# Streaming the first FFN's opening weights and the conditioning rows through one six-slot ring, with the first block accumulated row by row in eight PSUM banks

## The chip, the cores and the metric

The kernel runs on one Trainium2 chip, as one program on all eight NeuronCores (two dies of four). The metric is device time in microseconds of the slowest core. A program on all eight cores has a second, slower state in some executions, in which one die shows a lower granted clock (in one slow run of the changed kernel die 0 had 0.93 and the time was 1721.6 us). "Fast runs" means the rest. Ratios, means over cores and profiles use fast runs alone; the medians below count slow runs too.

TensorE is the matmul engine, ScalarE does activations, VectorE elementwise arithmetic, GpSimd simple elementwise work and casting DMAs, and SyncE issues plain DMAs. SBUF is a core's working memory, and PSUM, in eight banks, takes what TensorE writes. In profile lines they are PE, ACT, DVE, POOL and SP.

## The reference, cut to what matters

The block is a macaron: half an FFN, a token mixer, half an FFN. Each sub-layer is preceded by an RMS norm whose scale and shift come from a conditioning vector `c`.

```python
cc = jax.nn.silu(c)
mod = (cc @ w_ada[l] + b_ada[l]).reshape(b, N_ADA, D_MODEL)    # 9 vectors of 1024
sh1, sc1, gt1, sh2, sc2, gt2, sh3, sc3, gt3 = ...
h = rms_norm(x, g_ffn1[l]) * (1 + sc1) + sh1                   # modulated norm
x = x + 0.5 * gt1 * swiglu(h, w_ffn1_in[l], w_ffn1_out[l])     # first FFN, 1024 -> 2 x 2816 -> 1024
# ... token mixer (chunked attention and pooling), then the second FFN in the same form
```

Each core holds 2048 tokens and a halo of 512, as five blocks of 512 columns. All are transposed, so that the 1024 features lie on partitions, as eight tiles (`kt`) of 128. x, the weights and the conditioning matrix are float32 in HBM. Matmuls are bf16.

## The kernel before

Every instruction goes through a small recording layer, which finds dependences and sets semaphores. Each engine runs its own list in order. An instruction that waits also holds back everything behind it on its engine. (In the trace of the kernel before, ScalarE waits 13.19 us, until 80.91, for an x block that it is to square, and a Silu queued behind starts only at 82.82.)

A norm has a statistics part (`stats`: squares on ScalarE, column sums by matmul with a matrix of ones, Ln and Exp on ScalarE) and an apply part (`ap`, one per tile: a multiply on VectorE, then an add on ScalarE for even tiles and on VectorE for odd ones). Its output, `h`, is kept for each block as `H[b]`, the input of the FFN's matmuls:

```python
def norm_parts(b, sub, mode, out=None):
    ...                                            # cut
    def sq(p):
        return lambda: P.act(SQ[p % 2][:, :, :], x[:, 2 * p:2 * p + 2, :], AF.Square)
    def ln():
        P.act(r, sbk, AF.Ln, bias=EPSC[:, 0:1])
        P.act(r, r, AF.Exp, scale=-0.5)
    def ap(kt):
        def f():
            t = TMP[kt % 2]
            P.stt(t, x[:, kt, :], DER[:, 3 * sub, kt:kt + 1], r, ALU.mult, ALU.mult)
            if mode == "act" or (mode == "mix" and kt % 2 == 0):
                P.act(h[:, kt, :], t, AF.Identity, bias=DER[:, 3 * sub + 1, kt:kt + 1])
            else:
                P.ts(h[:, kt, :], t, DER[:, 3 * sub + 1, kt:kt + 1], ALU.add)
        return f
```

At the start, two x blocks and 16 rows of `w_ada` are loaded through SyncE's queue. Each row is turned into one scale or shift by a VectorE dot product. The first `w1i` tiles are loaded by GpSimd, which casts to bf16 in the DMA, and each of these loads waits for a given dot, so that it does not steal bandwidth from the rows. The third x block waits for the last of these loads:

```python
for i in range(16):
    dots.append(ada_dot(aorder[i], ADA_R[i % 6]))
    if i + 6 < 16:
        ada_load(aorder[i + 6], ADA_R[i % 6], "d_a%d" % (i % 6))
    ...                                            # cut: scale/shift, early H tiles of blocks 0 and 1
pre1, body1 = ffn(w1i, w1o, 0, [0, 1, 2, 3, 4], True, ..., startup=[dots[1], dots[7], dots[11], dots[13]], ...)
pre1()
last = pre1()
P.load("sp", XB[1][:, :, :], xT[2], "d_x2", deps=last)
```

A `unit` is 16 matmuls into a pair of PSUM banks (8 for each half of the SwiGLU), a Silu and a multiply. In "group 0" each of the five blocks has four units. The norms of blocks 2 to 4 are woven between the units of the blocks before them (`norm_slots`):

```python
def unit(k, jj, b, spread=None):
    ...                                            # cut: 16 matmuls into bank 2*pi and 2*pi+1
    P.act(s, bank(2 * pi), AF.Silu)
    P.tt(ACTB[jl][:, b, :], s, bank(2 * pi + 1), ALU.mult)

for bi, b in enumerate(blocks):                    # group 0
    for k in range(2):
        for jj in range(2):
            unit(k, jj, b, spread if bi == k == jj == 0 else None)
            side["g0"](bi, 2 * k + jj)             # parts of the norms of later blocks
```

## Time and profile before

| | before |
|---|---|
| time, median of 3 runs | 1636.98 us (1635.83 to 1641.05) |
| spans of the eight cores in the profiled run | 1622.4 to 1638.0 us |
| TensorE busy | 1517.3 us, 93% |

The page's first lines and its queue table (queue, kind: packets, MB written, share of the time of 16 DMA engines):

```profile
span 1638.0 us, 20449 instructions; the slowest of 8 cores (1622.4 to 1638.0 us)
...
PE 1517.3 (93%) x7085; PEld 669.1 (41%) x7085; DVE 821.3 (50%) x1300; ACT 478.9 (29%) x615; POOL 96.2 (6%) x193
...
q0 software_dynamic: 31184, 59.91, 22.4%
q1 hardware_dynamic: 14688, 58.30, 11.0%
```

Queue 0 casts float32 to bf16, so 59.91 MB written are 119.8 MB read.

The chain of waits of the kernel before, followed back from the last instruction, cut to 60 to 150 us (start, length, what was waited for or run; L179 and so on are the recording layer's lines):

```profile
58.42 6.86 DMA arena<-w1i
65.52 15.31 DMA arena<-xT
80.91 1.07 ACT arena L185
...
89.05 1.28 ACT L186
...
91.76 1.28 ACT L185
```

Read it as a relay. The chain waits 6.9 us for a casting weight load, then 15.3 us for the third x block (issued only at 65.5), then it follows ScalarE's norm work. ACT L186 and L185 with 1.28 us are loads of the activation table: Ln and Silu need different tables, so each norm swaps twice.

The stretches table of the kernel before, some of its rows (per stretch: length, busy us and count for each engine, then the granted TensorE clock, the DMA share and GB/s):

```profile
core 3: us, PE busy (x) PEld busy (x) DVE busy (x) ACT busy (x) POOL busy (x), PEclk, DMA share, GB/s
...
70.00:80.00 10.00, 0.15 (x1) 0.00 (x0) 0.00 (x0) 0.00 (x0) 0.00 (x0) 0.74 1.00 260
80.00:90.00 10.00, 7.89 (x30) 3.10 (x31) 1.37 (x2) 5.92 (x7) 0.00 (x0) 0.74 1.04 304
90.00:100.00 10.00, 9.56 (x46) 4.13 (x43) 5.00 (x8) 6.79 (x10) 0.00 (x0) 1.00 0.61 233
110.00:120.00 10.00, 7.88 (x37) 3.36 (x35) 7.11 (x11) 5.86 (x8) 0.00 (x0) 1.00 0.18 53
140.00:150.00 10.00, 6.58 (x22) 2.23 (x20) 5.96 (x10) 2.52 (x4) 0.00 (x0) 0.83 0.29 107
```

TensorE does next to nothing from 70 to 80 us, and from about 146 us on it is full but for some 2 us at the second FFN's entry and holes in the mixer. So the front is what a change can improve.

### The profile page before, as it was taken

The numbers are of one execution on the slowest core, as the hardware profiler recorded it, in microseconds if no ns is written. First come the engines' busy times: TensorE is split into PE (matmuls) and PEld (weight loads), VectorE is DVE, ScalarE is ACT, GpSimd is POOL, SyncE is SP. The second block draws the span as 40 slices with busy tenths as digits, with TensorE's granted clock in tenths as the row PEclk, the third lists the DMA queues.
The fourth block names the chain that finished last, engine by engine and source line by source line (L and its number), as shares of the span: only waits on it lengthen the run. The fifth ranks groups of instructions, "written<-read, shape, count | busy, mean of one in ns | idle before, by whom it ended". The sixth has DMA issues, their size and how long they took to land.

```text
span 1638.0 us, 20449 instructions; the slowest of 8 cores (1622.4 to 1638.0 us)
## 1 busy us (share of the span) xinstructions
PE 1517.3 (93%) x7085; PEld 669.1 (41%) x7085; DVE 821.3 (50%) x1300; ACT 478.9 (29%) x615; POOL 96.2 (6%) x193
## 2 busy tenths in 40 slices
PE   1488999999999999988699988799999999999999
PEld 0133444444444444343244433244434444444444
DVE  3446736537346346756555456455356261624326
ACT  3363010110110114657744157643250101010110
POOL 0101000010010000000100000111000000001000
PEclk9899999999999999999999999899999999999999
DMA  9844353151361344020144530344304313104005
GB/s 278 185 144 103 67 129 78 39 135 39 90 130 32 80 116 89 1 38 15 21 71 77 90 53 1 51 71 67 71 3 75 52 27 58 27 14 85 13 1 205
DMA packets 45970, 119.50 MB, mean 73 GB/s; under 512 B 4144, under 2 KB 4272, under 8 KB 45360
## 3 DMA queue, kind: packets, MB, share of 16 engines
q0 software_dynamic: 31184, 59.91, 22.4%
q1 hardware_dynamic: 14688, 58.30, 11.0%
q8 instruction: 60, 0.98, 0.2%
q14 instruction: 38, 0.31, 0.1%
HBM read 169.70 MB, written 8.39 MB: 109 GB/s over the span
## 4 chain that ended last, share of the span: by engine, by line
PE 82%; ACT 5%; DVE 5%; DMA 4%; issue 3%; SPq 0%; DVEq 0%; ACTq 0%; POOL 0%; POOLq 0%
PE ps L179 82%; ACT arena L185 3%; DVE arena L189 2%; DVE arena L194 1%; DMA arena<-w_ada 1%; ACT arena L186 1%; DMA arena<-w_ap 1%; DMA arena<-xT 1%; DVE arena L196 1%; SPq L215 0%; DMA arena<-w1i 0%; DVE arena L209 0%; DVE arena L201 0%; ACT L185 0%; ACT L186 0%
## 5 line engine op out<-in xcount | busy, mean ns | idle before, releaser
L179 PE MATMUL ps<-arena 128*128 128x512 bf16 (+3 forms) x7085 | 1517.3, 377 | 116.8 <-ACT arena L185 55.6
L179 PEld LDWEIGHTS ps<-arena 128*128 128x128 bf16 (+1 forms) x7085 | 669.1, 98 | 964.5 <-issue 212.0
L185 ACT ACTIVATE arena<-ps 128x512 bf16<-128x512 f32 (+4 forms) x368 | 270.3, 744 | 870.5 <-PE ps L179 862.1
L189 DVE TENSOR_TENSOR arena<-arena,ps 128x512 bf16<-128x512 bf16 (+1 forms) x230 | 175.2, 762 | 563.8 <-PE ps L179 484.6
L194 DVE SCALAR_TENSOR_TENSOR arena<-ps,arena 128x512 f32<-128x512 f32 (+1 forms) x410 | 315.8, 774 | 125.6 <-PE ps L179 71.1
L185 ACT ACTIVATE arena<-arena 128x1024 bf16<-128x1024 f32 (+2 forms) x105 | 95.2, 929 | 42.8 <-DMA arena<-xT 17.6
L189 DVE TENSOR_TENSOR arena<-arena 128x512 bf16<-128x512 bf16 (+10 forms) x191 | 89.9, 494 | 25.5 <-ACT arena L185 17.3
L196 DVE SCALAR_TENSOR_TENSOR arena<-arena 128x1024 f32<-128x1024 f32 x72 | 87.8, 1219 | 26.4 <-DMA arena<-w_ada 25.5
L186 ACT ACTIVATE arena<-arena 128x512 bf16<-128x512 f32 (+1 forms) x84 | 57.5, 714 | 121.1 <-DVE arena L194 96.4
L194 DVE SCALAR_TENSOR_TENSOR arena<-arena 128x512 f32<-128x512 f32 (+2 forms) x114 | 78.8, 727 | 6.2 <-ACT arena L186 2.9
L215 POOL DMA_DIRECT2D arena<-w1i x28 | 17.8, 636 | 517.2 <-PE ps L179 463.3
L189 DVE TENSOR_TENSOR arena<-ps,arena 64x512 bf16<-64x512 f32 x32 | 22.0, 689 | 35.0 <-ACT arena L185 31.5
L215 POOL DMA_DIRECT2D arena<-w3i x24 | 16.2, 677 | 380.3 <-PE ps L179 380.3
L215 POOL DMA_DIRECT2D arena<-w_in x28 | 19.8, 707 | 306.8 <-PE ps L179 289.4
L186 ACT ACTIVATE arena<-ps,arena 128x1024 f32<-128x1024 f32 (+1 forms) x32 | 29.6, 925 | 25.5 <-PE ps L179 25.3
L185 ACT ACT_TABLE_LOAD x14 | 18.0, 1283 | 43.6 <-PE ps L179 36.5
L201 DVE TENSOR_SCALAR arena<-arena 128x512 bf16<-128x512 f32 (+2 forms) x45 | 19.9, 443 | 5.7 <-DMA arena<-cst 1.1
L186 ACT ACT_TABLE_LOAD x12 | 15.4, 1283 | 16.3 <-PE ps L179 16.2
L212 POOL MEMSET arena<- 64x128 bf16 x64 | 11.8, 197 | 132.1 <-ACT arena L185 132.1
L201 DVE TENSOR_SCALAR arena<-ps,arena 128x512 bf16<-128x512 f32 (+2 forms) x25 | 15.7, 644 | 7.2 <-PE ps L179 7.0
L209 DVE CAST arena<-ps 128x256 bf16<-128x256 f32 x32 | 12.1, 419 | 7.4 <-PE ps L179 7.4
L209 DVE COPY arena<-arena 128x16 f32<-128x16 f32 (+2 forms) x35 | 6.0, 171 | 8.2 <-ACT arena L185 6.8
(14 smaller groups left out, 51.1 us busy)
## 6 DMA issues: line engine op xcount, KB each, us to landing
arena<-w_ada SPq DMA_DIRECT2D x72, 512.0 KB, 4.4
arena<-w_in POOLq DMA_DIRECT2D x28, 512.0 KB, 6.7
arena<-w3i POOLq DMA_DIRECT2D x20, 512.0 KB, 6.8
arena<-w1i POOLq DMA_DIRECT2D x16, 512.0 KB, 8.9
outT<-arena SPq DMA_DIRECT2D x16, 512.0 KB, 2.9
arena<-xT SPq DMA_DIRECT2D x3, 2048.0 KB, 23.4
arena<-w1o POOLq DMA_DIRECT2D x10, 512.0 KB, 15.1
arena<-w3o POOLq DMA_DIRECT2D x10, 512.0 KB, 9.8
```

The lines of the kernel that those rows point to most:

```text
L179: return self.op("pe", lambda e: e.matmul(out, lhsT=lhsT, rhs=rhs, start=start, stop=stop), reads=[lhsT, rhs], writes=[out])
L185: return self.op("act", lambda e: e.activation(out=out, in_=in_, func=func, scale=scale), r, [out])
L186: return self.op("act", lambda e: e.activation(out=out, in_=in_, func=func, bias=bias, scale=scale), r, [out])
L189: return self.op(eng, lambda e: e.tensor_tensor(out=out, in0=in0, in1=in1, op=op), [in0, in1], [out])
L194: return self.op("dve", lambda e: e.scalar_tensor_tensor(out=out, in0=in0, scalar=scalar, in1=in1, op0=op0, op1=op1), r, [out])
L196: return self.op("dve", lambda e: e.scalar_tensor_tensor(out=out, in0=in0, scalar=scalar, in1=in1, op0=op0, op1=op1, accum_out=accum), r, ...
L201: return self.op(eng, lambda e: e.tensor_scalar(out=out, in0=in0, scalar1=s1, scalar2=None, op0=op0), r, [out])
L209: return self.op(eng, lambda e: e.tensor_copy(out=out, in_=in_), [in_], [out])
L212: return self.op(eng, lambda e: e.memset(out, v), [], [out])
L215: return self.op(q, lambda e: e.dma_start(out=out, in_=in_), [], [out], deps, sem)
```

## The change

The intent has four parts. (1) One hardware queue carries x blocks 0 and 1 and then, through a ring of six slots, eight weight tiles in float32 and the 16 conditioning rows. ScalarE casts the weight tiles. (2) As each pair of rows becomes a scale and a shift, one H tile of block 0 is made and all four units of block 0 take their eight matmuls of that tile at once, in all eight PSUM banks. After the last row, block 0 is nearly done. Dummy ("warm") matmuls fill the gaps. (3) The norms of blocks 2 to 4 do their four squares together, with four buffers. (4) Their odd-tile adds go to GpSimd, in the second FFN too. (One more edit, not in this list: the conditioning dots among these norms, which prepare later scales and shifts, stand behind units 0, 2 and 3 of a block and no longer behind 0, 1 and 2.)

The diff, cut to its core:

```diff
+    RING = [view(o_h + 16384 + 4096 * i, F32, (D,)) for i in range(6)]
+    tiles = [w1i[half * NJ + j] for j in range(4) for half in (0, 1)]
+    tiles += [w_ada[8 * (1 - s_) + k] for k in range(8) for s_ in (0, 1)]
+    def tile_load():
+        n = tn[0]
+        if n < len(tiles):
+            tn[0] += 1
+            P.load("sp", RING[n % 6], tiles[n], "d_a%d" % (n % 6))
...
+    for j in range(4):
+        for half in range(2):
+            n = 2 * j + half
+            P.act(piece((0, 2)[j // 2] + half)[:, j % 2, :], RING[n % 6], AF.Copy)
+            tile_load()
+    P.act(EPSC[:, 1:2], EPSC[:, 0:1], AF.Silu)
     for i in range(16):
-        dots.append(ada_dot(aorder[i], ADA_R[i % 6]))
+        slot = RING[(8 + i) % 6]
+        P.stt(slot, slot, 1.0, CB[:, :], ALU.mult, ALU.mult, accum=MRAW[...])
+        if i == 0:
+            warm(10, 0, True, P.q["dve"][-1])
+        tile_load()
         if i % 2 == 1:
...
+            for b in range(2):
+                P.act(H[b][:, kt, :], XR[b][:, kt, :], AF.Identity, scale=..., bias=...)
+            for j in range(4):
+                for half in range(2):
+                    P.mm(bank(2 * j + half), piece(...)[:, j % 2, kt * 128:(kt + 1) * 128], H[0][:, kt, :],
+                         kt == 0, kt == 7)
+            if kt < 7:
+                warm(5, 7, False)
...
-                if mode == "act" or (mode == "mix" and kt % 2 == 0):
+                if mode == "act" or (mode != "dve" and kt % 2 == 0):
                     P.act(h[:, kt, :], t, AF.Identity, bias=DER[:, 3 * sub + 1, kt:kt + 1])
                 else:
-                    P.ts(h[:, kt, :], t, DER[:, 3 * sub + 1, kt:kt + 1], ALU.add)
+                    P.ts(h[:, kt, :], t, DER[:, 3 * sub + 1, kt:kt + 1], ALU.add, "pool" if mode == "pool" else "dve")
...
-    N1 = norm_slots(2, 3, 0, 2)
+    for b in range(2, 5):
+        st, ap = norm_parts(b, 0, "pool", sq4, tmp4)
+        at = (4, 5, 5, 6, 7) if b == 2 else (4 * b - 5, 4 * b - 4, 4 * b - 4, 4 * b - 3, 4 * b - 2)
+        for v, f in zip(at, (st[:4], st[4:], ap[:3], ap[3:6], ap[6:])):
+            N1.setdefault(v, []).extend(f)
...
-    P.load("sp", XB[1][:, :, :], xT[2], "d_x2", deps=last)
+    for b in range(2, 5):
+        for p in range(4):
+            P.load("sp", XB[b - 1][:, 2 * p:2 * p + 2, :], xT[b][:, 2 * p:2 * p + 2, :], "d_x%d%d" % (b, p))
...
```

More of the change, by code (lines that the diff above doesn't have):

```diff
@@ L417, in build_nc, with norm_parts @@
     nctr = [0]
-    def norm_parts(b, sub, mode, out=None):
+    def norm_parts(b, sub, mode, sqs=None, tmps=None):
         i = nctr[0]
@@ L424, in norm_parts @@
         x = xb(b)
-        h = H[b] if out is None else out
+        h = H[b]
+        sqs = SQ if sqs is None else sqs
+        ns = len(sqs)
+        tmps = TMP if tmps is None else tmps
         def sq(p):
-            return lambda: P.act(SQ[p % 2][:, :, :], x[:, 2 * p:2 * p + 2, :], AF.Square)
+            return lambda: P.act(sqs[p % ns][:, :, :], x[:, 2 * p:2 * p + 2, :], AF.Square)
         def st(p):
@@ L432, in f @@
                 for q in range(2):
-                    P.mm(sbk, ONES[:, :], SQ[p % 2][:, q, :], p == 0 and q == 0, p == 3 and q == 1)
+                    P.mm(sbk, ONES[:, :], sqs[p % ns][:, q, :], p == 0 and q == 0, p == 3 and q == 1)
             return f
@@ L441, in f @@
             def f():
-                t = TMP[kt % 2]
+                t = tmps[kt % len(tmps)]
                 P.stt(t, x[:, kt, :], DER[:, 3 * sub, kt:kt + 1], r, ALU.mult, ALU.mult)
-                if mode == "act" or (mode == "mix" and kt % 2 == 0):
+                if mode == "act" or (mode != "dve" and kt % 2 == 0):
                     P.act(h[:, kt, :], t, AF.Identity, bias=DER[:, 3 * sub + 1, kt:kt + 1])
                 else:
-                    P.ts(h[:, kt, :], t, DER[:, 3 * sub + 1, kt:kt + 1], ALU.add)
+                    P.ts(h[:, kt, :], t, DER[:, 3 * sub + 1, kt:kt + 1], ALU.add, "pool" if mode == "pool" else "dve")
             return f
         stats = [sq(0), sq(1), st(0), sq(2), st(1), sq(3), st(2), st(3), ln]
+        if ns == 4:
+            stats = [sq(p) for p in range(4)] + [st(p) for p in range(4)] + [ln]
         return stats, [ap(kt) for kt in range(8)]
@@ L471, in build_nc @@
     P.load("sp", CB[:, :], cb_d, "d_cb")
-    ADA_R = [view(o_h + 16384 + 4096 * i, F32, (D,)) for i in range(6)]
+    RING = [view(o_h + 16384 + 4096 * i, F32, (D,)) for i in range(6)]
     XR = [view(base + 17408, F32, (8, TB)), view(o_w + 4 * 4096, F32, (8, TB))]
-    aorder = [8 * (1 - s) + k for k in range(8) for s in (0, 1)]
+    tiles = [w1i[half * NJ + j] for j in range(4) for half in (0, 1)]
+    tiles += [w_ada[8 * (1 - s_) + k] for k in range(8) for s_ in (0, 1)]
+    tn = [0]
+    def tile_load():
[3 more added lines that the diff above has]
+            P.load("sp", RING[n % 6], tiles[n], "d_a%d" % (n % 6))
     for b in range(2):
@@ L477, in build_nc @@
             P.load("sp", xb(b)[:, 2 * p:2 * p + 2, :], xT[b][:, 2 * p:2 * p + 2, :], "d_x%d%d" % (b, p))
-        if b == 0:
-            for i in range(2):
-                ada_load(aorder[i], ADA_R[i], "d_a%d" % i)
-    for i in range(2, 6):
-        ada_load(aorder[i], ADA_R[i], "d_a%d" % i)
+    for i in range(6):
+        tile_load()
     P.memset(ONES[:, :], 1.0 / 1024.0)
@@ L492, in build_nc, with warm @@
     P.ts(B1, CST[:, 16:24], 1.0, ALU.add)
-    def warm(n):
+    def warm(n, bk, start, after=None):
         for _ in range(n):
-            P.mm(bank(5), WARM[:, 0:128], WARM[:, :], True, True)
-    def xr_parts(b):
+            P.op("pe", lambda e: e.matmul(bank(bk), lhsT=WARM[:, 0:128], rhs=WARM[:, :], start=start, stop=start),
+                 [WARM[:, :]], [bank(bk)], [after])
+    for b in range(2):
         st, _ = norm_parts(b, 0, "mix")
-        r = RSTD[b]
-        return st, [lambda kt=kt: P.tt(XR[b][:, kt, :], xb(b)[:, kt, :], r, ALU.mult) for kt in range(8)]
-    st0, xr0 = xr_parts(0)
-    st1, xr1 = xr_parts(1)
-    seq = {0: st0[:2], 1: st0[2:3] + st0[3:6], 2: st0[6:], 3: xr0[0:2], 4: xr0[2:4] + st1[:2], 5: xr0[4:6] + st1[2:6],
-           6: xr0[6:8] + st1[6:], 7: xr1[0:2], 8: xr1[2:4], 9: xr1[4:6], 10: xr1[6:8]}
-    dots = []
-    def early(b, kt):
-        P.act(H[b][:, kt, :], XR[b][:, kt, :], AF.Identity, scale=DER[:, 0, kt:kt + 1], bias=DER[:, 1, kt:kt + 1])
-    eseq = {7: [(0, 0), (0, 1), (0, 2), (0, 3)], 9: [(0, 4)], 11: [(0, 5), (1, 0), (1, 1)], 13: [(0, 6), (1, 2), (1, 3)],
-            15: [(0, 7), (1, 4), (1, 5), (1, 6), (1, 7)]}
-    for i in range(16):
-        dots.append(ada_dot(aorder[i], ADA_R[i % 6]))
-        if i + 6 < 16:
-            ada_load(aorder[i + 6], ADA_R[i % 6], "d_a%d" % (i % 6))
+        for f in st:
+            f()
+        for kt in range(8):
+            P.tt(XR[b][:, kt, :], xb(b)[:, kt, :], RSTD[b], ALU.mult)
+    for j in range(4):
[4 more added lines that the diff above has]
+    P.act(EPSC[:, 1:2], EPSC[:, 0:1], AF.Silu)
+    P.ts(EPSC[:, 2:3], EPSC[:, 0:1], EPSC[:, 0:1], ALU.add, "pool")
+    for i in range(16):
+        slot = RING[(8 + i) % 6]
+        P.stt(slot, slot, 1.0, CB[:, :], ALU.mult, ALU.mult, accum=MRAW[:, 8 * (1 - i % 2) + i // 2:8 * (1 - i % 2) + i // 2 + 1])
+        if i == 0:
+            warm(10, 0, True, P.q["dve"][-1])
+        tile_load()
         if i % 2 == 1:
@@ L520, in build_nc @@
             P.tt(DER[:, 1, kt:kt + 1], MRAW[:, kt:kt + 1], CST[:, 8 + kt:9 + kt], ALU.add)
-        for f in seq.get(i, []):
-            f()
-        for b, kt in eseq.get(i, []):
-            early(b, kt)
+            for b in range(2):
+                P.act(H[b][:, kt, :], XR[b][:, kt, :], AF.Identity, scale=DER[:, 0, kt:kt + 1], bias=DER[:, 1, kt:kt + 1])
+            for j in range(4):
+                for half in range(2):
+                    P.mm(bank(2 * j + half), piece((0, 2)[j // 2] + half)[:, j % 2, kt * 128:(kt + 1) * 128], H[0][:, kt, :],
+                         kt == 0, kt == 7)
+            if kt < 7:
+                warm(5, 7, False)
     ada_j = [16]
@@ L540, in build_nc, with ffn, wi_load @@
     G0 = [sum(GS[:g]) for g in range(5)]
-    def ffn(w_i, w_o_, sub, blocks, first, side, wi_slots, wo_odd, startup=None, tail=None, spread=None):
+    def ffn(w_i, w_o_, sub, blocks, side, wi_slots, wo_odd, started=False, tail=None):
         chunks = [(g, c) for g in range(5) for c in range((GS[g] + 1) // 2)]
         nload = [0]
-        def wi_load(split=None):
+        def wi_load():
             k = nload[0]
@@ L554, in wi_load @@
             sa, sb = wi_slots[k % 2]
-            if split is not None:
-                return [P.load("pool", piece(s)[:, jj:jj + 1, :],
-                               w_i[o + j0 + jj:o + j0 + jj + 1].rearrange("j p c -> p j c"),
-                               "d_w%d" % s if jj == 0 else "d_wy%d" % s, deps=[split[2 * k + jj]])
-                        for jj in range(nt) for s, o in ((sa, 0), (sb, NJ))]
             for s, o in ((sa, 0), (sb, NJ)):
@@ L562, in ffn, with unit @@
         ucnt = [0]
-        def unit(k, jj, b, spread=None):
+        def unit(k, jj, b, done=None):
             g, c = chunks[k]
@@ L567, in unit @@
             jl = 2 * c + jj
-            pi = nextpair()
-            order = [(s, o, kt) for s, o in ((sa, 0), (sb, 1)) for kt in range(8)]
-            if spread is not None:
-                order.sort(key=lambda x: x[2])
-            for s, o, kt in order:
-                P.mm(bank(2 * pi + o), piece(s)[:, jj, kt * 128:(kt + 1) * 128], H[b][:, kt, :], kt == 0, kt == 7)
-                if spread is not None and o == 1:
-                    spread(kt)
+            pi = nextpair() if done is None else done
+            if done is None:
+                for s, o in ((sa, 0), (sb, 1)):
+                    for kt in range(8):
+                        P.mm(bank(2 * pi + o), piece(s)[:, jj, kt * 128:(kt + 1) * 128], H[b][:, kt, :], kt == 0, kt == 7)
             s = SA[ucnt[0] % 2]
@@ L607, in pre @@
         def pre():
-            return wi_load(startup)
+            return wi_load()
         def body():
-            if startup is None:
+            if started:
+                nload[0] = 2
+                for u in range(4):
+                    unit(u // 2, u % 2, blocks[0], done=u)
+            else:
                 wi_load()
@@ L614, in body @@
             for bi, b in enumerate(blocks):
+                if bi == 0 and started:
+                    continue
                 for k in range(2):
                     for jj in range(2):
-                        unit(k, jj, b, spread if bi == k == jj == 0 else None)
+                        unit(k, jj, b)
                         side["g0"](bi, 2 * k + jj)
@@ L642, in ffn, with norm_slots @@
         return pre, body
-    def norm_slots(first, nb, sub, start):
+    def norm_slots(first, nb, sub, start, lo=0):
         slots = {}
@@ L649, in put @@
             slots.setdefault(v, []).extend(f)
-        free_at = 0
+        free_at = lo
         for q in range(nb):
@@ L654, in norm_slots @@
             v = [v0, v0 + 1, v0 + 2]
-            st, ap = norm_parts(first + q, sub, "mix")
+            st, ap = norm_parts(first + q, sub, "pool")
             put(v[0], st[0], st[1])
@@ L667, in g0_norms @@
             f()
-    N1 = norm_slots(2, 3, 0, 2)
+    N1 = {}
+    sq4 = SQ + [view(o_w + 4 * 4096 + 2048 * i, BF16, (2, TB)) for i in range(2)]
+    tmp4 = TMP + [view(o_w + 5 * 4096 + 2048 * i, F32, (TB,)) for i in range(2)]
+    for b in range(2, 5):
[3 more added lines that the diff above has]
+            N1.setdefault(v, []).extend(f)
     sd = Side()
-    pend = []
-    for b in range(1, 5):
-        pend.append(None)
     ucount = [0]
@@ L678, in g0_1 @@
         g0_norms(4 * bi + u, N1)
-        if bi >= 2 and u < 3:
+        if bi >= 2 and u != 1:
             ada_step()
@@ L710, in tail_1 @@
                 tl[b].q.extend(ng)
-    pre1, body1 = ffn(w1i, w1o, 0, [0, 1, 2, 3, 4], True, dict(g0=g0_1, g0end=g0end_1, unit=unit_1, op=lambda: None),
-                      [(0, 1), (2, 3)], (4, 5), startup=[dots[1], dots[7], dots[11], dots[13]], tail=tail_1,
-                      spread=lambda kt: warm(5) if 2 <= kt <= 6 else None)
-    pre1()
-    last = pre1()
-    P.load("sp", XB[1][:, :, :], xT[2], "d_x2", deps=last)
-    for i in range(2):
-        ada_load(16 + i, ada_slot(16 + i), "d_b%d" % i)
-    for b in range(3, 5):
-        P.load("sp", XB[b - 1][:, :, :], xT[b], "d_x%d" % b)
-    P.load("pool", WPG[:, :, :], w_pg.rearrange("(g c) d -> c g d", c=128), "d_wpg", deps=[dots[15]])
+    _, body1 = ffn(w1i, w1o, 0, [0, 1, 2, 3, 4], dict(g0=g0_1, g0end=g0end_1, unit=unit_1, op=lambda: None),
+                   [(0, 1), (2, 3)], (4, 5), started=True, tail=tail_1)
+    for b in range(2, 5):
+        for p in range(4):
+            P.load("sp", XB[b - 1][:, 2 * p:2 * p + 2, :], xT[b][:, 2 * p:2 * p + 2, :], "d_x%d%d" % (b, p))
+        if b == 2:
+            for i in range(2):
+                ada_load(16 + i, ada_slot(16 + i), "d_b%d" % i)
+    P.load("pool", WPG[:, :, :], w_pg.rearrange("(g c) d -> c g d", c=128), "d_wpg", deps=[P.q["dve"][-1]])
     body1()
@@ L1036, in build_nc @@
     sl = fr[:2] + rest
-    pre2, body2 = ffn(w3i, w3o, 2, [1, 2, 3, 4], False, dict(g0=g0_2, g0end=sd2.drain, unit=lambda: None, op=lambda: None),
+    pre2, body2 = ffn(w3i, w3o, 2, [1, 2, 3, 4], dict(g0=g0_2, g0end=sd2.drain, unit=lambda: None, op=lambda: None),
                       [(sl[0], sl[1]), (sl[2], sl[3])], (sl[4], sl[5]), tail=tail_2)
```

## The prediction

> **What bounds the kernel now.** The page has TensorE busy 1517 of 1638 us (93%); the stretches table shows it full from about 146 us on, but for 2 us near 1200 to 1220. Only the front is worth anything. There TensorE is busy 9.2 us of 60 to 70, 0.15 of 70 to 80, 7.9 of 80 to 90, 6.6 of 140 to 150. The chain of waits names, in order: conditioning rows by DMA to 31 us; VectorE dots and XR products to 57; DMA of w1i to 65; DMA of the third x block from 65.5 to 80.9 (held until the last w1i load is issued); then a ScalarE/VectorE norm chain of 19 to 20 us a block (table loads at 91.8, 110.7, 130.6). Block 0's last unit ends at about 87 us, block 4's H is complete at 146, group 0 ends at about 158.5.
>
> **What changes.**
> - Removed: eight casting w1i loads that waited for dots. They now stream ahead of the rows. By the queue table a casting byte read costs the DMA engines no more (59.9 MB written, so 119.8 read, took 22.4%; 58.3 MB plain took 11.0%). The Trainium skill, "DMA: Bandwidth & Descriptors" (SWDGE vs HWDGE vs iDMA), has casts only on the GpSimd path; hence 8 ScalarE casts, about 1.0 us each, hidden under DMA.
> - Moved: two x blocks, 8 weight tiles and 16 rows are 17.4 MB in one queue. The trace had moved 11.0 MB by 40 us and then ran at 318 GB/s: last row at about 60 us (estimate). First row at about 35; two dots with scale and shift take 3.53 us (54.72 to 58.25), eight pairs 28: last dot at about 63, against 60.8. Six slots hold 10 us of stream, issue to landing takes 4.4: the ring should not starve.
> - Gained: after the last row 8 matmuls remain, not 3 units, and the third x block lands at about 68, not 81. Block 1 starts at about 67, against 87.
> - Norms of blocks 2 to 4: four squares (4 us), 8 statistics matmuls (1.75), Ln with table (2.0), Exp 0.63, 8 applies, odd adds on GpSimd. The skill's "GPSIMD Engine Reference" (Engine selection) calls one-input ops there roughly line-rate; estimate 0.8 to 1.2 us against 0.49 on VectorE; the trace of before has none. Walking the in-order queues with the trace's durations (silu 0.6, multiply 0.69, apply 0.7, add 0.72, dot 1.3), H of blocks 2, 3, 4 is complete 27, 45 and 64 us after the last dot: still 18 to 19 us a block, not TensorE's 16, as Silu and Ln still swap tables.
> - Group 0 then ends at 63+77=140, against 158.5.
>
> **On the critical path.** Nearly all 18 us. About 1 us may come or go at the second FFN, whose adds also go to GpSimd. Warm matmuls fill gaps: free.
>
> **Prediction:** 1637-18 = 1619 us, 8 in 10 between 1611 and 1627. Over 2% faster 0.04 (TensorE-bound from 67 us would save only about 30 us), within 2% 0.95, over 2% slower 0.01.
>
> **Right or wrong if** (timeline): last row's dot at 60 to 66 us; silu within 3 us of it; no TensorE hole over 5 us between 66 and 80; block 2's squares at 69 to 74; first output projection at 136 to 145; table loads still 18 to 20 us apart; the rest unchanged within 2 us.
>
> **What would make it wrong.** The ring starves: last dot after 68. GpSimd adds over 2 us, or VectorE slowed beside them. The w1o loads delay x. Better: blocks come every 16 us, up to 28 us saved. Worse: block 1 waits over 2 us for pair 0's eviction.

## The result, and the profile after

| | before | changed |
|---|---|---|
| median, same rounds | 1638.53 us | 1634.51 us |
| ratio of fast runs | | 0.9973, 95% interval 0.9949 to 0.9998 |
| slowest core of the profiled run | 1638.0 us (core 3) | 1633.7 us (core 4) |
| mean of the eight cores, profiled run | 1628.5 us | 1627.3 us |

A ratio is the mean time of one kernel's fast runs over that of the other's of the same rounds, so it is not quite the ratio of the medians. The change gains 0.3%. 1619 was predicted, and the measured time is above the range.

Three marks serve below, each read from the traces of all eight cores. Mark A is the moment TensorE restarts for good on block 4's first unit in group 0. Mark B is the length from the Silu table load that opens the second FFN to the same restart there. Mark C is the start of the last Silu of group 0; it is the best one, since it exists whatever the holes look like.

| mean of 8 cores (range) | before | changed |
|---|---|---|
| squares of block 2 start | 75.8 us (72.8 to 81.1) | 70.9 us (70.0 to 72.0) |
| mark A | 141.4 us (137.7 to 146.2) | 137.2 us (135.6 to 138.3) |
| mark C | 154.8 us (151.0 to 159.5) | 149.8 us (147.9 to 151.4) |
| mark B | 48.3 us | 51.0 us |

So the front gains 4.9 us on the mean core, and the second FFN's entry loses 2.7. Between the two, from mark C to the second FFN's opening, the mean core took about 1 us longer (1007.9 before, 1009.0 changed). That leaves the 1.2 us of the table. The slowest core gained more, 4.3 us; a likely reason, not tested, is that before the cores' fronts were scattered over 8.5 us and now lie within 3.5.

The page of the changed kernel, its head and its new group (line, engine, operation, shapes, count, busy us and mean ns of one, idle before):

```profile
span 1633.7 us, 20428 instructions; the slowest of 8 cores (1622.2 to 1633.7 us)
...
PE 1515.0 (93%) x6965; PEld 672.2 (41%) x7105; DVE 812.8 (50%) x1280; ACT 487.1 (30%) x624; POOL 133.8 (8%) x206
...
L201 POOL TENSOR_SCALAR arena<-arena 128x512 bf16<-128x512 f32 (+1 forms) x21 | 40.6, 1938 | 114.4 <-DVE arena L194 77.7
```

The line to see is the third: the new GpSimd adds take 1938 ns on average. The VectorE form of the same add, by the groups of the kernel before from 80 to 146 us, took 486:

```profile
L201 DVE TENSOR_SCALAR arena<-arena 128x512 bf16<-128x512 f32 x12 | 5.8, 486 | 1.3
```

The chain of waits of the changed kernel from 60 to 150 us, cut (short pieces of "issue" between the lines are left out too):

```profile
66.31 7.07 PE ps L179 x32
...
76.97 1.28 ACT L186
...
88.70 1.83 POOL arena L201
90.80 1.57 POOL arena L201
92.50 5.26 PE ps L179 x17
97.82 1.28 ACT L186
...
109.53 1.83 POOL arena L201
111.62 2.26 POOL arena L201
114.02 7.71 PE ps L179 x23
```

The long waits for weights and for x are gone. In their place the chain goes through GpSimd (POOL L201) at the end of each block's norm, and then through TensorE stretches that are long for their count: 17 matmuls in 5.26 us are 309 ns each, where a run of 32 before the hole took 7.07 us, 221 ns each.

The stretches table of the changed kernel, some of its rows:

```profile
core 4: us, PE busy (x) PEld busy (x) DVE busy (x) ACT busy (x) POOL busy (x), PEclk, DMA share, GB/s
...
70.00:80.00 10.00, 9.95 (x47) 4.58 (x47) 1.90 (x4) 7.46 (x9) 0.00 (x0) 1.00 1.06 265
80.00:90.00 10.00, 5.18 (x22) 1.98 (x21) 6.43 (x10) 4.97 (x7) 5.69 (x3) 0.93 1.00 233
90.00:100.00 10.00, 8.52 (x31) 3.33 (x32) 1.17 (x2) 6.62 (x9) 2.35 (x2) 0.73 0.11 31
110.00:120.00 10.00, 6.86 (x20) 2.44 (x19) 4.88 (x8) 5.47 (x7) 3.87 (x2) 0.66 0.31 106
```

The stretch 70 to 80 is full, as intended. But look at the granted clock: 0.73 from 90 to 100 and 0.66 from 110 to 120, where the kernel before had 1.00. (That kernel had its own slow stretches, 0.74 from 70 to 90, where TensorE had little to do at first, and 0.83 from 140 to 150.)

### The profile page after: what moved, and what is told of

Its sections match the earlier page's. It is cut to its first block, busy times and chain, and to the rows that moved or that the text cites. A ratio compares the mean times of both kernels' runs of the same rounds, so it can differ in the third digit from the quotient of the medians.

```text
span 1633.7 us, 20428 instructions; the slowest of 8 cores (1622.2 to 1633.7 us)
## 1 busy us (share of the span) xinstructions
PE 1515.0 (93%) x6965; PEld 672.2 (41%) x7105; DVE 812.8 (50%) x1280; ACT 487.1 (30%) x624; POOL 133.8 (8%) x206
## 4 chain that ended last, share of the span: by engine, by line
PE 82%; DVE 5%; ACT 5%; issue 4%; DMA 2%; POOL 1%; DVEq 0%; SPq 0%; ACTq 0%; POOLq 0%
PE ps L179 82%; ACT arena L185 3%; DVE arena L194 2%; DVE arena L189 2%; POOL arena L201 1%; DVE arena L196 1%; DMA arena<-w_ap 1%; ACT arena L186 1%; DMA arena<-xT 1%; DMA arena<-w_ada 1%; ACT L186 0%; DVE arena L209 0%; ACT L185 0%; DVE arena L201 0%; DVE arena L212 0%
## 5 line engine op out<-in xcount | busy, mean ns | idle before, releaser
L179 PE MATMUL ps<-arena 128*128 128x512 bf16 (+5 forms) x6922 | 1503.8, 377 | 102.4 <-ACT arena L185 38.3
L185 ACT ACTIVATE arena<-arena 128x1024 bf16<-128x1024 f32 (+2 forms) x114 | 102.5, 930 | 29.4 <-PE ps L179 16.0
L201 POOL TENSOR_SCALAR arena<-arena 128x512 bf16<-128x512 f32 (+1 forms) x21 | 40.6, 1938 | 114.4 <-DVE arena L194 77.7
L215 POOL DMA_DIRECT2D arena<-w1i x20 | 13.6, 681 | 383.2 <-PE ps L179 383.2
L506 PE MATMUL ps<-arena 128*128 128x512 bf16 x43 | 12.4, 423 | 12.4 <-DVE arena L196 12.3
L201 DVE TENSOR_SCALAR arena<-ps,arena 128x512 bf16<-128x512 f32 (+2 forms) x25 | 15.7, 644 | 5.7 <-PE ps L179 5.4
```

What stands on the lines that cost most here:

```text
L179: return self.op("pe", lambda e: e.matmul(out, lhsT=lhsT, rhs=rhs, start=start, stop=stop), reads=[lhsT, rhs], writes=[out])
L185: return self.op("act", lambda e: e.activation(out=out, in_=in_, func=func, scale=scale), r, [out])
L201: return self.op(eng, lambda e: e.tensor_scalar(out=out, in0=in0, scalar1=s1, scalar2=None, op0=op0), r, [out])
L215: return self.op(q, lambda e: e.dma_start(out=out, in_=in_), [], [out], deps, sem)
L506: P.op("pe", lambda e: e.matmul(bank(bk), lhsT=WARM[:, 0:128], rhs=WARM[:, :], start=start, stop=start), [WARM[:, :]], [bank(bk)], [after])
```

## The experiments

Theory 1 was that GpSimd adds are slower than I had estimated and stretch every norm. Its first rival, theory 2, was that the grouped order of squares and statistics sets the spacing. Theories 1b and 3 concern what the front's gain came from; theory 4, the clock, arose from the first results. All results, in the order of the runs (mark C from each profiled run; "mean core" is the mean over cores and fast runs, for before 1631.1 to 1632.3 us):

| run | ratio to before (95%) | median us | mark C | mark B | mean core |
|---|---|---|---|---|---|
| changed kernel | 0.9973 (0.9949 to 0.9998) | 1634.5 | 149.8 | 51.0 | 1627.0 |
| e1 adds on VectorE | 0.9935 (0.9919 to 0.9951) | 1627.6 | 146.4 | 48.3 | 1621.4 |
| e2 the same, first FFN only | 0.9951 (0.9936 to 0.9967) | 1630.3 | 146.6 | 51.2 | 1623.9 |
| e3 before, adds on GpSimd | 1.0067 (1.0020 to 1.0113) | 1657.6 | 157.4 | 51.0 | 1635.3 |
| e4 before, third x block early | 1.0003 (0.9980 to 1.0026) | 1640.2 | 154.6 | 48.3 | 1630.7 |
| e5 e1 with warm matmuls in holes | 0.9902 (0.9863 to 0.9942) | 1626.6 | 142.1 | 48.3 | 1619.5 |
| e6 e1 with early squares | 0.9878 (0.9835 to 0.9921) | 1622.8 | 138.3 | 48.3 | 1615.8 |
| e8 e1 with the old norm order | 0.9937 (0.9888 to 0.9986) | 1632.4 | 148.9 | 48.3 | 1624.8 |
| e9 e6 with warm matmuls in hole | 0.9896 (0.9881 to 0.9911) | 1622.9 | 137.2 | 48.3 | 1615.5 |
| e10 changed, warm in holes | 0.9981 (0.9962 to 0.9999) | 1636.5 | 145.0 | 51.2 | 1625.9 |
| e11 changed, no stream warm | 1.0010 (0.9987 to 1.0032) | 1642.7 | 150.1 | 51.4 | 1630.4 |
| e12 changed, again | 0.9941 (0.9895 to 0.9986) | 1633.4 | 149.8 | 51.1 | 1627.1 |
| e13 e10 again | 0.9947 (0.9887 to 1.0007) | 1637.7 | 144.0 | 51.4 | 1623.6 |
| e14 e6 again | 0.9885 (0.9828 to 0.9941) | 1624.4 | 137.8 | 48.3 | 1616.3 |

Medians count slow runs too (e1, e3, e4 and e13 had two each, the changed kernel, e6, e8, e11 and e14 one). e7 was a single look and is told below. The groups e1 to e4, e5 to e8, e9 to e11 and e12 to e14 each ran on a chip of their own, so a run of one group is compared with a run of another by its marks, its mean core and its ratio, across chips. For the changed kernel that is safe: its mark C and mean core came out the same in two calls (149.8 twice, 1627.0 and 1627.1). All outputs were correct.

Read the ratios with one caution. Some runs that count as fast have two cores at a clock of 0.96 to 0.97 and take about 15 us more. There are two such among e3's four fast runs, two among the ten of the kernel before in e5 to e8, and two among its eleven in e12 to e14. Without them e3's ratio is 1.0014 in place of 1.0067, and the ratios of e5, e6, e8, e12 and e14 are about 0.002 higher (0.9922, 0.9898, 0.9957, 0.9963 and 0.9906). No order of kernels below rests on them, but e3's size does.

On the chip of e9 to e11 the four cores of die 0 were at times granted a clock of 0.81, in runs that count as fast. No other run's trace shows it. Here is one stretch of e11 (columns as in the stretches tables above), first on core 2, then on core 6; the clock is the third number from the end:

```profile
621.00:636.00 15.00, 15.00 (x59) 6.20 (x57) 8.05 (x11) 2.00 (x2) 0.00 (x0) 0.81 0.56 91
```

```profile
621.00:636.00 15.00, 14.29 (x66) 6.30 (x65) 10.07 (x16) 6.79 (x11) 0.00 (x0) 1.00 0.32 54
```

For these three runs the cores of die 1, which were not disturbed, are the ones to read.

### e1: the adds back on VectorE

```diff
-        st, ap = norm_parts(b, 0, "pool", sq4, tmp4)
+        st, ap = norm_parts(b, 0, "mix", sq4, tmp4)
...
-            st, ap = norm_parts(first + q, sub, "pool")
+            st, ap = norm_parts(first + q, sub, "mix")
```

> The changed kernel with the odd-tile adds of both FFNs back on VectorE, nothing else. Mark A: the moment TensorE restarts for good on block 4's first unit in group 0, mean of the eight cores (before 141.4 us, changed 137.2). Mark B: from the Silu table load that opens the second FFN to the same restart there (before 48.3 us, changed 51.0). Theory 1 (GpSimd adds of 1.6 to 3.1 us stretch every norm): mark A 129 to 132, mark B 48.3, time 0.5 to 0.7% below the changed kernel, about 1625 us, ratio to before about 0.992. Theory 2 (the grouped squares and statistics set the 21 to 23 us spacing of blocks whatever does the adds): mark A 135 or later, mark B 48.3, ratio to before about 0.996.

Mark A was 133.4, between the two theories. Mark B returned exactly to 48.3. The time fell to 1627.6. So theory 1 holds for 3.4 us of mark C and all 2.7 us of the second FFN, but it is not the whole, since the walk through the queues had promised more.

### e2: the adds of the first FFN alone on VectorE

The first of e1's two edits alone.

> The changed kernel with the adds of the first FFN alone on VectorE; the second FFN keeps GpSimd. Theory 1: mark A as in the run with both (129 to 132 us), mark B stays 51.0, time 2.5 to 3 us above that run (about 1627 us): the second FFN's share of the cost is separate and additive. Theory 2: mark A 135 or later, time within 2 us of the changed kernel.

Mark A 133.6, mark B 51.2, and 2.5 us more than e1 on the mean core. The two places add up, as theory 1 says.

### e3: the kernel before, with the adds on GpSimd

```diff
-            st, ap = norm_parts(first + q, sub, "mix")
+            st, ap = norm_parts(first + q, sub, "pool")     # odd adds on GpSimd, as in the change
```

> The kernel before, with only the odd-tile adds of blocks 2 to 4 and of the second FFN moved to GpSimd. Theory 1: the adds take 1.6 to 3 us here too, mark A moves from 141.4 to 145 to 149, mark B from 48.3 to 51.0, time 6 to 10 us longer, ratio to before 1.004 to 1.006. Theory 2: in the old, spread schedule the adds are hidden in the first FFN, mark A within 1.5 us of 141.4; only mark B grows, ratio about 1.002.

Mark A 145.5, mark B 51.0, ratio 1.0067. In the second FFN the adds cost the same 2.7 us as in the change. In the first they cost less: block 2's squares started 1.6 us later in this profile, by the x block's arrival, so of mark A's 4.1 us only about 2.5 are the adds', and of mark C's 2.6 us only about 1.0, against 3.4 in the changed kernel. The old, spread order hides most of them. The ratio fits theory 1, but half of it rests on the two runs with two slow cores named above; without them it is 1.0014, and the mean core is 2.1 us slower and not 4.2. So this run lies between the two theories.

### e4: the kernel before, with the third x block early

```diff
-    P.load("sp", XB[1][:, :, :], xT[2], "d_x2", deps=last)
+    for p in range(4):
+        P.load("sp", XB[1][:, 2 * p:2 * p + 2, :], xT[2][:, 2 * p:2 * p + 2, :], "d_x2%d" % p)
```

> The kernel before, with only the load of the third x block freed from its wait for the last casting w1i load: four quarter loads issued right behind the conditioning rows. Casting loads, ring, block 0 all as before. Theory 1b (what the change gained in front is that the third x block lands earlier, as the norm chain of blocks 2 to 4 starts there; block 0's early end itself is worth nothing): squares of block 2 start at 66 to 71 us instead of 73 to 81, mark A falls from 141.4 to 135 to 138, time 4 to 8 us below before, ratio 0.995 to 0.9975, as good as the whole change. Theory 3 (block 0 accumulated during the stream is what gains): the early x block competes with the casting w1i loads, block 0 ends later, mark A 140 or later, ratio 0.999 or more.

The squares started at 67.4 us instead of 75.8, but mark A stayed at 141.6 and the time at 1.0003. Theory 1b, that the earlier x block by itself is the gain, falls. TensorE's timeline of this run shows why: with x ahead of them the last casting weight loads land late, and block 0 waits for weights.

```profile
75.03 1.89 PE L179 MATMUL ps<-arena 128*128 128x512 bf16 x8 [3.04 <-DMA arena<-w1i]
81.81 16.67 PE L179 MATMUL ps<-arena 128*128 128x512 bf16 x62 [4.89 <-DMA arena<-w1i]
```

So moving x forward alone did not help, as the weights then came late; the ring moves both. Whether accumulating block 0 during the stream (theory 3) gains anything beyond the earlier weights, no run tested.

### e5: e1 with dummy matmuls in the holes

```diff
+                        if fill is not None and o == 0:
+                            for _ in range(({2: 10, 3: 4, 5: 10} if fill == 6 and b == 2 else {3: 3, 5: 9}).get(kt, 0)):
+                                P.mm(bank(fill), ONES[:, :], H[0][:, 0, :], True, True)
```

`fill` is the statistics bank that is not in use, given for the first unit of blocks 2 to 4 only.

> The kernel with all adds on VectorE, plus dummy matmuls (24 for block 2, 12 for blocks 3 and 4) inside the first unit of blocks 2, 3 and 4, where TensorE waits for H tiles. Theory 4 (the rest of the gap to the predicted 140 is the clock: after each hole the granted clock falls to 0.5 to 0.6 and the unit and the next block's statistics run at 427 ns a matmul, which delays Ln by about 3 us a block): the granted clock stays at 1.0 between 84 and 140 us, the Ln table load follows the restart of TensorE by 3.6 us instead of 7.0, mark A falls from 133.4 to 127 to 130, time 3 to 6 us below the run with all adds on VectorE, about 1623 us. Rival (the chain of ScalarE and VectorE sets the spacing, whatever the clock): mark A 132.5 or later, time within 1.5 us of that run.

Stretches of e1, at 88 to 96 and 112 to 120 us (same columns as above):

```profile
88.00:92.00 4.00, 1.38 (x4) 0.31 (x3) 3.64 (x7) 2.35 (x4) 0.00 (x0) 0.50 0.53 134
92.00:96.00 4.00, 4.00 (x11) 1.40 (x11) 0.02 (x1) 3.84 (x5) 0.00 (x0) 0.50 0.02 5
...
112.00:116.00 4.00, 2.61 (x9) 1.05 (x10) 3.89 (x7) 3.54 (x5) 0.00 (x0) 0.82 0.01 2
116.00:120.00 4.00, 4.00 (x16) 1.58 (x15) 1.19 (x3) 2.57 (x4) 0.00 (x0) 0.75 0.69 227
```

The same stretches of e5:

```profile
88.00:92.00 4.00, 3.88 (x17) 1.61 (x18) 2.85 (x5) 2.45 (x4) 0.00 (x0) 1.00 0.46 130
92.00:96.00 4.00, 4.00 (x19) 1.68 (x18) 0.69 (x1) 3.66 (x5) 0.00 (x0) 1.00 0.01 2
...
112.00:116.00 4.00, 3.65 (x17) 1.43 (x16) 1.74 (x3) 3.67 (x5) 0.00 (x0) 1.00 0.72 213
116.00:120.00 4.00, 3.95 (x20) 1.80 (x19) 2.26 (x4) 2.13 (x4) 0.00 (x0) 1.00 0.14 55
```

In e1 the clock is at half after block 2's hole: 11 matmuls in 4 us. In e5 it is 1.00 throughout, and mark C falls by 4.3 us to 142.1. Theory 4 holds in the front. The median fell by only 1 us, which by itself would fit the rival, and the mean core by 1.9: the later stages gave the rest back (see below).

### e6: e1 with early squares

```diff
-        at = (4, 5, 5, 6, 7) if b == 2 else (4 * b - 5, 4 * b - 4, 4 * b - 4, 4 * b - 3, 4 * b - 2)
-        for v, f in zip(at, (st[:4], st[4:], ap[:3], ap[3:6], ap[6:])):
+        w = 4 * b - 4
+        at = (4, 4, 5, 5, 6) if b == 2 else (w - 2, w - 1, w, w, w + 1)
+        for v, f in zip(at, (st[:2], st[2:4], st[4:], ap[:4], ap[4:])):
             N1.setdefault(v, []).extend(f)
```

> The kernel with all adds on VectorE, with the squares of blocks 3 and 4 issued in pairs in the two units before their statistics and the applies in two batches of four instead of three. Theory 2 (squares serial behind the previous block's applies cost 3 to 4 us a block): Ln of blocks 3 and 4 comes earlier, mark A 128 to 131. If the clock alone is at fault, mark A stays within 1.5 us of 133.4, as the first unit of a block still runs at half clock after its hole.

Mark C fell by 8.1 us to 138.3, the time to 1622.8. ScalarE's timeline of e6 at the Ln table loads of blocks 2, 3 and 4:

```profile
77.42 1.28 ACT L186 ACT_TABLE_LOAD   x1 [1.97 <-PE ps L179]
...
96.92 1.28 ACT L186 ACT_TABLE_LOAD   x1 [2.35 <-PE ps L179]
...
114.86 1.28 ACT L186 ACT_TABLE_LOAD   x1 [0.33 <-PE ps L179]
```

They are 19.5 and 17.9 us apart. In the changed kernel they were at 76.97, 97.82 and 120.51, so 20.9 and 22.7 apart; in e1 21.6 and 20.7; in e5 19.1 and 19.5 (each on its slowest core). The order does two things at once: squares no longer stand behind the previous block's applies, and the holes before blocks 3 and 4 shrink below 1 us, so the clock stays up there. This run does not part the two, but e5 and e9 do, since neither has any stretch at half clock from 84 to 140 us. With the clock full in both, what parts their mark C is the order: 142.0 against 137.0 on the cores of die 1, so 5 us (on two chips). That leaves about 3 of the 8.1 us to the clock. The run beats both kernels: 0.9878 of before.

### e7: no dots beside the GpSimd adds

```diff
-        if bi >= 2 and u != 1:
-            ada_step()
```

> The changed kernel (adds on GpSimd) with no conditioning dots among the norms of group 0: all eight dots come at its end. If a GpSimd add is stretched by a VectorE instruction with two SBUF inputs that runs beside it, the adds of 3.06 us, which lie beside a dot, fall to 1.6 to 2.0 us and no add is above 2.4 us; if 3.06 us is a property of the add itself (its buffers), it stays. Mark A moves little either way (135 to 138); the dots at the end cost time, so this run's total says nothing.

GpSimd's timeline of the changed kernel first, then of e7:

```profile
81.40 1.90 POOL L201 TENSOR_SCALAR arena<-arena 128x512 bf16<-128x512 f32 x1 [13.14 <-DVE arena L194]
86.22 6.14 POOL L201 TENSOR_SCALAR arena<-arena 128x512 bf16<-128x512 f32 x3 [2.92 <-DVE arena L194]
102.21 3.06 POOL L201 TENSOR_SCALAR arena<-arena 128x512 bf16<-128x512 f32 x1 [9.86 <-DVE arena L194]
107.04 6.83 POOL L201 TENSOR_SCALAR arena<-arena 128x512 bf16<-128x512 f32 x3 [1.77 <-DVE arena L194]
```

```profile
103.55 1.93 POOL L201 TENSOR_SCALAR arena<-arena 128x512 bf16<-128x512 f32 x1 [9.38 <-DVE arena L194]
108.38 6.14 POOL L201 TENSOR_SCALAR arena<-arena 128x512 bf16<-128x512 f32 x3 [2.90 <-DVE arena L194]
```

The lone add of a block, 3.06 us where a multiply and a dot run beside it, fell to 1.93; three adds take 6.14 in place of 6.83. One by one these three are now 2.51, 2.11 and 1.56 us. So the foretold "no add is above 2.4 us" was missed: the add of 2.51 us, with two multiplies beside it, stays. Mark A, 134.9, was just below the foretold range. In the second FFN, where fewer VectorE instructions run beside them, eight adds of the changed kernel took 1562 ns each:

```profile
L201 POOL TENSOR_SCALAR arena<-arena 128x512 bf16<-128x512 f32 x8 | 12.5, 1562 | 37.2 <-DVE arena L194 37.2
```

So an add costs about 1.56 us with little beside it, 1.90 to 2.51 beside one or two of VectorE's multiplies and 3.06 beside a multiply and a dot. The Trainium skill, "GPSIMD Engine Reference" (Specifications), says that GpSimd's SBUF interfaces contend with VectorE instructions that have two SBUF inputs, and both the multiply and the dot have two. "SBUF — State Buffer" (Who interferes with whom) calls the shared ports an exclusive lock. The trace agrees as far as it goes: a dot of 1.22 us lengthens the lone add by 1.13 us (3.06 against 1.93). And on core 4 the five adds of blocks 2 and 3 that start while such a VectorE instruction runs end 1.34 to 1.43 us after it ends (after the second, where two follow each other), while an add alone takes 1.56. The run took 1662.6 us in all, because its dots stand at the end of group 0, as foretold.

### e8: e1 with the old order of norms

```diff
+    N1 = norm_slots(2, 3, 0, 2, 4)       # in place of the grouped loop of the change; mode "mix"
```

> The kernel with all adds on VectorE and the old order of norms (two square buffers, squares and statistics spread over three units) in place of the grouped one, from the same start. If grouping squares and statistics is what opens the holes and halves the clock: spacing of blocks 18.6 to 20 us as in the kernel before, granted clock 1.0 through blocks 3 and 4, mark A 129 to 132, time 1 to 4 us below the run with all adds on VectorE. If grouping helps as intended: mark A 135 to 138, time 2 to 5 us above.

Mark C 148.9, which is 2.5 us later than e1. The grouping helps, as intended; the clock fell to 0.50 to 0.57 in places here too. Theory 2 in its strong form, that grouping itself is the harm, falls.

### e9: e6 with dummy matmuls in the one long hole

The fill of e5 with `{3: 12, 5: 5}` for block 2 alone.

> Mark C: start of the last Silu of group 0, mean of the eight cores (before 154.8 us, changed 149.8, adds on VectorE 146.4, that with dummy matmuls in the holes 142.1, that with early squares instead 138.3). This run is early squares plus 17 dummy matmuls in the one long hole that is left, in block 2's first unit. Clock theory: granted clock 1.0 from 84 to 140 us, mark C 135 to 137 (block 3's Ln load at 94 to 95 us instead of 96.9). Time 1 to 3 us below the run with early squares (1622.8), about 1621, unless the later stages give it back: in that run the stretch after mark C was already 3 to 4 us longer on the mean core than in the changed kernel with the adds on VectorE. If the clock does not matter with early squares: mark C within 1 us of 138.3.

Mark C 137.2 (137.0 on die 1), 1.1 us earlier than e6: just outside both ranges that were foretold. The median, 1622.9, is the same, but die 0 was slowed here; the cores of die 1 took 1614.3 us on average, against 1615.8 for the mean core of e6. So the fill is worth about 1.5 us at most.

### e10: the changed kernel with dummy matmuls in its holes

The fill of e5 with `{2: 19, 4: 8, 6: 5}` for block 2 and `{2: 4, 4: 6, 6: 6}` for blocks 3 and 4.

> The changed kernel with its GpSimd adds kept, plus dummy matmuls in the holes of the first units of blocks 2 to 4 (32, 16, 16). If the two costs, GpSimd adds and half clock, are separate terms: mark C falls from 149.8 by about 4 us, as it did with the adds on VectorE (146.4 to 142.1), to 145 to 147, time about 1630. If the slow clock is only a consequence hidden behind the slow adds: mark C stays within 1.5 us of 149.8.

Mark C fell by 4.8 us to 145.0, so the two terms add in the front. The time did not show it: 0.9981, on a chip where the changed kernel had not been timed. Hence e12 and e13. Die 0's clock of 0.81 accounts for it (7 us lost on its mean core in the profiled run): the cores of die 1 took 1622.5 us on average over the fast runs, 8.6 less than those of the kernel before, and those of die 0 1629.3.

### e11: the changed kernel without its stream dummies

```diff
-            warm(10, 0, True, P.q["dve"][-1])
+            pass
...
-                warm(5, 7, False)
+                pass
```

> The changed kernel without its 45 dummy matmuls between the conditioning rows. If they are what holds the clock up during the stream: granted clock 0.5 to 0.6 in the stretch 40 to 66 us, eight matmuls of the last row take 3.4 us instead of 1.9, and block 1 starts at half clock: mark C 2 to 4 us later (152 to 154), time 2 to 4 us longer. If the eight real matmuls per 3.5 us keep the clock up by themselves: clock 1.0, mark C and time unchanged within 1 us.

Stretches of e11 in the row stream:

```profile
40.00:44.00 4.00, 2.15 (x6) 0.81 (x7) 3.26 (x9) 1.52 (x2) 0.00 (x0) 0.50 1.03 331
44.00:48.00 4.00, 3.09 (x12) 0.95 (x10) 2.87 (x7) 1.52 (x2) 0.00 (x0) 0.89 0.98 325
48.00:52.00 4.00, 1.89 (x8) 0.71 (x8) 3.15 (x8) 1.54 (x3) 0.00 (x0) 1.00 0.99 315
```

The clock is at half only until the second row pair, then 1.00, with TensorE busy 1.9 of 4 us. Mark C is 150.1. The 45 dummy matmuls do nothing that is needed here. The run's time, 1642.7, is higher, but only by die 0, at 0.81 in places: its cores took 1633.8 us on average over the fast runs, those of die 1 1627.1, as the mean core of the changed kernel.

### e12, e13, e14: the changed kernel, e10 and e6 on one chip

No new edits.

> The changed kernel as it is, on the chip of the two runs that follow. If chips differ in how much the later stages give back: its ratio to before is 0.997 to 1.002 here, and only differences within this call count. Mark C 149 to 151 us.

> The changed kernel with its holes filled by dummy matmuls, as in the earlier run. If the clock is a term of its own: mark C 4 to 5 us before that of the changed kernel in this call and the time 3 to 6 us below it (ratio lower by 0.002 to 0.0035). If the later stages give it back: mark C earlier, time within 1.5 us of the changed kernel.

> Adds on VectorE and early squares, as in the earlier run. Mark C 11 to 12 us before that of the changed kernel and 2.7 us less at the second FFN's entry: 14 us at most. If the later stages keep it: time 12 to 14 us below the changed kernel in this call; as the earlier runs suggest they give back 3 to 4 us: 9 to 12 us below, ratio to before 0.987 to 0.991.

The changed kernel's mark C was 149.8 again and its mean core 1627.1. Its ratio, 0.9941, missed the foretold 0.997 to 1.002 on the fast side; without the two runs of the kernel before with slow cores it is 0.9963, just below. Filling the holes brought mark C to 144.0 and the mean core to 1623.6, so 3.5 of 5.8 us reach the mean core's total. The slowest core's gain is not shown: 1632.1 us on average for the changed kernel, 1633.2 for the filled one, or 1630.5 without the one run whose core 0 had a clock of 0.966. e14 has mark C 137.8, mean core 1616.3 and a mean of fast runs of 1624.3 us, against 1633.6 for the changed kernel: 9.4 us faster on one chip, within the foretold 9 to 12.

Where do the later stages give it back? From mark C to the second FFN's opening the mean core took 1009.0 us in the changed kernel, 1008.9 in e1, but 1010.9 in e5, 1012.3 in e6, 1013.2 in e9; on one chip, 1009.0 in e12, 1010.2 in e13 and 1012.6 in e14. The granted clock there is below 1 in short episodes, on every core, mostly in the mixer (from 638 to 1055 us on core 4 of the changed kernel). Counted from 140 to 1600 us, as the sum of the lost share of each 20 us stretch, they are 16.8 us a core in the changed kernel and 17.4 in e1, but 19.3 in e6 and 21.1 in e9 (0.7 of these by die 0's clock of 0.81); 17.7 in e12, 21.3 in e13 and 19.7 in e14. So part of the loss goes with more time at a lower clock. Why an earlier front brings more of it is not settled.

## Why the prediction was wrong

Right:
- The bottleneck and the stream. The ring did not starve. The last dot ended at 64.8 us on the mean core, against 63 foretold; Silu followed within 3 us (66.79 after 64.54 on core 4); no hole above 0.6 us between 66 and 80; block 2's squares at 70 to 72.
- The third x block was freed together with the weights; freed alone it gained nothing (e4).
- GpSimd adds over 2 us were named as a way to be wrong. That is what happened.

Wrong, by the terms of its sum. It had group 0 end at 140 us. Read as the end of the last matmul, that is mark C at about 138.3 (the last unit's second half of eight matmuls, 1.7 us, lies between). Mark C was 149.8, so 11.5 us late. Terms 1 and 2 are the steps that failed:
1. **The GpSimd add**, "estimate 0.8 to 1.2 us". Measured 1.56 alone, 1.9 to 3.06 beside VectorE work, 2.33 on average in group 0. It cost 3.4 us of mark C (e1) and all 2.7 us at the second FFN, where the prediction had "about 1 us may come or go". The skill's "roughly line-rate" was taken for a duration, though the same row names VectorE for elementwise adds. The same page's other statements, on contention with two-input VectorE instructions, were not used.
2. **The walk of the queues** ("H of blocks 2, 3, 4 is complete 27, 45 and 64 us after the last dot"). On core 4 it was 27.8, 49.3 and 72.0. The walk had every matmul at full clock (its "8 statistics matmuls (1.75)" are 219 ns each). But its own "18 to 19 us a block, not TensorE's 16" leaves TensorE idle for 2 to 3 us a block, and after the holes the granted clock fell to half: the rest of the unit and the next block's eight statistics matmuls, which the next Ln waits for, ran at up to 427 ns. This term was left out wholly. Removing it is worth 4.3 us of mark C in e1 (e5) and 4.8 to 5.8 in the changed kernel (e10, e13). The Trainium skill, "TensorE: Matmul & The Clock Gate" (What's actually happening), describes the fall to half clock when TensorE idles; the trace agrees (0.50 from 114 to 118 us, after the holes before block 3).
3. **The last dot**, 1.8 us later than estimated.
4. About 2 us remain (11.5 less 3.4, 4.3 and 1.8), which no experiment was made for. They depend on the reading of "140": if it meant mark C itself, as the 158.5 beside it nearly did (core 3's mark C is 159.2), the shortfall is 9.8 us and 0.3 remain.

That e6 arrived at 138.3 all the same is chance, as it did so with another order of squares than the prediction's.

A further error is in the baseline. The 158.5 us was read from core 3, the slowest. The mean core's mark C was 154.8, so 4.4 us of the "18 us" (159.2 less 154.8) were core 3's own late x block (80.9 us against a mean of 75.8) and not there to be gained by the others. The time is that of the slowest core, and which core that is depends on the later stages too: in the changed kernel it is core 4, whose mark B begins 1027 us after mark A, the longest of the eight.

The prediction's signs tell the same: first output projection on VectorE at 152.6 us, not 136 to 145; table loads 20.9 and 22.7 us apart, not 18 to 20; the second FFN not within 2 us.

## What to carry to other kernels

When you walk in-order queues by hand, give TensorE a clock: where your own walk leaves it idle for several us, at once or in holes close together, cost the next matmuls at half speed too, and look at what waits for them. Not every hole does it: in the kernel before, one of 2.12 us at 117.55 left the clock at 1.00. Before moving an elementwise operation to another engine because that engine is idle, measure it beside its neighbours: an idle engine with a duration three to six times as long, at the end of a chain, is not a relief. Read marks on all cores, not on the slowest one alone, before you say how much there is to gain.

## What the Trainium skill lacked or had wrong

- "GPSIMD Engine Reference", Engine selection: calls one-input elementwise work on GpSimd roughly line-rate. A one-input add of 128x512, float32 to bf16, took 1.56 us with little beside it, against 0.49 on VectorE, 3.2 times as long. (The row is right that such adds belong on VectorE.)
- The same page, Specifications: names the contention with VectorE instructions of two SBUF inputs but gives no size. Here an add grew from 1.56 to 1.90 to 2.51 us beside multiplies and to 3.06 beside a multiply and a 1.22 us dot.
- "TensorE: Matmul & The Clock Gate", HAM oscillation: gives as the rule no idle gap over about 3.4 us. Here shorter ones sufficed when they came close together: in the changed kernel holes of 0.94, 1.50 and 1.64 us before block 3, with two matmuls between each, were followed by a clock of 0.50 (114 to 118 us). The page's next section tells of frequent small idle times that do the same, but gives no size for them. TensorE busy 1.9 of 4 us in even portions kept 1.00 (e11).
- "ScalarE: Activation LUTs", What ACT_TABLE_LOAD costs: puts a switch at about 2.66 us, a load of 1.28 and a drain of 1.38. The load agrees (1.28), but the drain is not seen: in the changed kernel one activation ends at 82.69 us, the load starts at 82.70, and the next activation starts at 84.00.
